# Output projection of a hybrid decoder layer: weight tiles loaded unsplit up to the fifth last, and split by ScalarE and GpSimd from the third quarter on

## The chip, the cores and the metric

The kernel runs on one core of one Trainium2 chip. The metric is the device time of one execution in microseconds; the time given for a kernel is the median of several executions. A second figure, the span, is the time from the first to the last instruction of the one execution that the hardware profiler recorded.

The engines are called TensorE (PE in the profile; PEld is its weight load), VectorE (DVE), ScalarE (ACT), GpSimd (POOL) and SyncE (SP, here the queue that issues the DMAs). In the code they are `PE`, `V`, `S`, `G` and `nc.sync`.

## The reference

One decoder layer over 2048 tokens of width 1024, in fp32. What matters here is its middle:

```python
mix = concatenate([o_a, o_b])                    # two token mixers, (2048, 1024)
mix_out = einsum('btc,cd->btd', mix, w_out)      # the output projection
h = h + rms_norm(mix_out, post_mix_norm)
u = einsum('btd,df->btf', rms_norm(h, pre_mlp_norm), w_mlp_up)
y = einsum('btf,fd->btd', square(relu(u)), w_mlp_down)
h = h + rms_norm(y, post_mlp_norm)
```

Ahead of it stand an input projection and the mixers (a gated DeltaNet and an HGRN2), behind it the MLP and a gated embedding of 256 inputs.

## The kernel before

Activations lie transposed, with 128 channels on the partitions. The 2048 tokens are cut into four quarters `q` of 512 (`QT`), the 1024 channels into eight blocks `d` of 128 (`KD = 8`).

**Precision by splitting.** A product in fp32 is made of three products of rounded halves. Each operand x is stored as a tile of two halves: half 0 is x rounded to the format fp32r, half 1 is x minus half 0, rounded too. `split` (L157 to L160) makes them: ScalarE copies (L159), then another engine subtracts (L160), which is VectorE in all the calls of the output projection. One output tile (q, d) is 8 blocks of channels times 3 terms, 24 matmuls of 128x128 by 128x512. The first two terms of a block use half 0 of the weights, the third uses half 1.

**Weights of the output projection.** `order` (L321) lists the 32 tiles (q, d), quarter by quarter; j counts them. Each tile needs the weights of its d, so each d's weights are used four times, once per quarter. They come in two ways. `stage_out(j)` (L324) loads the unsplit weights, 128x1024 fp32 or 512 KB, into a buffer tagged `raw`, of which there are two; `ready_out(j)` (L330) then splits them into a buffer tagged `whl`, of which there are three. Or, if nothing was staged for j, `ready_out(j)` calls `reload` (L178), a load of 1 MB of split weights from a copy in DRAM, which `keep` (L172) wrote in the first quarter. Before the change the first three quarters (`RAW = 3`, j = 0 to 23) take the first way and the last quarter (j = 24 to 31) the second; all eight d are kept in the first quarter.

**The loop.** At L1283 the kernel goes over `order`. At the head of pass j it calls

```python
ready_out(j + 2)
stage_out(j + 3)
```

so weights are loaded three tiles ahead and split two tiles ahead. In pass j = 27 (`len(order) - 5`) it allocates two more tiles tagged `raw`, called `u_raw`, and loads into them the first weights of the MLP; their splits (`w_u`) follow in the last passes. After the product of a tile ScalarE copies the accumulator out (`yo`, L1319) and squares it into a buffer `sq` that exists once (L222); VectorE adds the square up (`acc_o`, L223). Four accumulators (`pp`) take turns.

**Work between the tiles.** `mm` (L1085) counts matmuls, and every eighth calls `tick`, which runs what the agenda has for that moment. So the small steps are placed by TensorE's count, not by time. They are: the splits of the activations of the next quarters (`mixT`, L212 and L213); and, for each finished quarter, `normed` (L1169): the norm of the projected tile (`hl_o`, `nrm_o`, then Ln and Exp on ScalarE, `r_o`), then `residual` (L1148) with its eight steps on VectorE (`yo` L1159 and L1160, with `xo` loaded and `h1d` stored), the sum of squares of the result (`sq_h`, `acc_h`), and its norm (`hl_h`, `nrm_h` L1121 and L1122, `rn`). The offsets of these steps are

```python
OUT_STEPS = (1, 5) + tuple(range(7, 15)) + (15, 25)
```

so the last of them, with the matmul `nrm_h` of the second quarter, comes at the 25th tick after that quarter, 200 matmuls on. From the norm of the second quarter follow the operands of the MLP (`early_operands` L1211 with `be`, `up_operands` L1222 with `b` and `t`), which the first matmul `u` after the loop needs.

**Order on the engines.** TensorE's order is the program's (`manual_schedule`, L300). SP's order is the program's up to the first outs of this projection (L1002) and again in the MLP (L1335); within the loop, and on VectorE, ScalarE and GpSimd everywhere, the framework sorts the instructions at build time. Each engine then works through its own list in order.

Of the kernel before, what the change touches and what calls it, by code (L numbers as in the profile page):

```python
# [23 lines left out]
KD = D // P  # L24
# [59 lines left out]
def trunk(ctx, tc, x, xT, pT, vecs, w_in, w_ab, gdn_a_log, gdn_dt_bias, w_out, w_up, w_down,  # L84
          w_ple, w_gate, consts, out):
    nc = tc.nc
    V, S, G, PE = nc.vector, nc.scalar, nc.gpsimd, nc.tensor
# [69 lines left out]
    def split(t, eng, raw):  # L157

        S.activation(t[:, 0], raw, AF.Copy)  # L159
        eng.tensor_tensor(t[:, 1], raw, t[:, 0], ALU.subtract)  # L160
# [11 lines left out]
    def keep(key, w):  # L172

        c = dr.tile([P, 2 * KD * P], F32, name=f"cache_{key}")
        nc.sync.dma_start(c, w.bitcast(F32).rearrange("p h k n -> p (h k n)"))
        cached[key] = c

    def reload(key, name):  # L178
        w = wp.tile([P, 2, KD, P], F32R, tag="whl", name=f"w_{name}")
        nc.sync.dma_start(w.bitcast(F32).rearrange("p h k n -> p (h k n)"), cached[key])  # L180
        return w
# [137 lines left out]
            yield  # L319

    order = [(q, d) for q in range(NQ) for d in range(KD)]  # L321
    staged_out, ready, RAW = {}, {}, 3

    def stage_out(j):  # L324
        if j < len(order) and order[j][0] < RAW:
            raw = wp.tile([P, KD, P], F32, tag="raw", name=f"raw_out{j}", bufs=2)
            nc.sync.dma_start(raw, w_out[order[j][1]])
            staged_out[j] = raw

    def ready_out(j):  # L330
        if j >= len(order):
            return
        if j not in staged_out:
            ready[j] = reload(f"out{order[j][1]}", f"out{j}")
            return
        ready[j] = wp.tile([P, 2, KD, P], F32R, tag="whl", name=f"w_out{j}")
        split(ready[j], V, staged_out.pop(j))
        if order[j][0] == 0:
            keep(f"out{order[j][1]}", ready[j])

    clock, agenda = [0], {}
# [54 lines left out]
    with mixers as mctx:  # L396
# [605 lines left out]
        with tc.manual_schedule(engines={mybir.EngineType.SP}):  # L1002
# [29 lines left out]
            accs, store = {q: None for q in qs}, None  # L1032
            at(clock[0], mix_operands(0), (1, 2, 3, 4, 6, 7, 9, 11))
            call(clock[0] + 2, partial(stage_out, 0))
            call(clock[0] + 5, partial(ready_out, 0))
            call(clock[0] + 6, partial(stage_out, 1))
            call(clock[0] + 13, partial(ready_out, 1))
            call(clock[0] + 14, partial(stage_out, 2))
            held = {}

# [242 lines left out]
    for j, (q, d) in enumerate(order):  # L1283
        if d == 0:
# [3 lines left out]
            if q == 1:  # L1288
                later(mix_operands(3), range(17, 25))
        ready_out(j + 2)  # L1290
        stage_out(j + 3)
        if j == len(order) - 5:
# [441 lines left out]
```

## Time and profile before

| | |
|---|---|
| median of 3 runs | 2773.16 us (2772.43 to 2774.76) |
| the profiled execution | 2769.21 us, its span 2767.3 us |
| TensorE / VectorE / ScalarE / GpSimd busy | 97% / 74% / 53% / 4% of the span |
| mean granted TensorE clock | 0.993 of full speed |
| output projection: first to last matmul `mmo` | 1131.5 to 1327.1 us |
| `w_out` split by ScalarE / VectorE | 24 times, 1057 / 1224 ns median |

In the tables of stretches each engine's busy time stands with its count of instructions in this order: PE, PEld, DVE, ACT, POOL; then the granted clock of TensorE, the share of the DMA engines and GB/s. In a timeline a row has its start, its length, engine, line, operation, output and inputs, shape and count; in brackets the idle time of the engine before it and what ended that. Rows of consecutive like instructions are merged. A row of one tile's instructions gives the durations as minimum / median / maximum in ns. A row of waits gives the total in us, the times and the longest.

### The profile page before, as it was taken

The numbers are of one execution on the slowest core, as the hardware profiler recorded it, in microseconds if no ns is written. First come the engines' busy times: TensorE is split into PE (matmuls) and PEld (weight loads), VectorE is DVE, ScalarE is ACT, GpSimd is POOL, SyncE is SP. The second block draws the span as 40 slices with busy tenths as digits, with TensorE's granted clock in tenths as the row PEclk, the third lists the DMA queues.
The fourth block names the chain that finished last, engine by engine and source line by source line (L and its number), as shares of the span: only waits on it lengthen the run. The fifth ranks groups of instructions, "written<-read, shape, count | busy, mean of one in ns | idle before, by whom it ended". The sixth has DMA issues, their size and how long they took to land.

```text
span 2767.3 us, 38374 instructions
## 1 busy us (share of the span) xinstructions
PE 2680.7 (97%) x12721; PEld 2215.3 (80%) x12721; DVE 2044.9 (74%) x4242; ACT 1469.9 (53%) x2943; POOL 104.2 (4%) x104
## 2 busy tenths in 40 slices
PE   6999999999999999999999999999999999999999
PEld 4788788788888887777788888887888888887887
DVE  6788877787787677578889867857787765567775
ACT  6665555455546445575555646545454445465431
POOL 0000000000000000000000000001000000001000
PEclk9999999999999999999999999999999999999999
DMA  7776777667666665887466447667454356577663
GB/s 261 255 250 217 235 247 247 219 209 250 220 213 202 214 227 170 278 276 258 140 214 224 172 175 237 225 193 239 157 191 162 135 175 203 194 254 240 214 206 121
DMA packets 268598, 589.24 MB, mean 213 GB/s; under 512 B 55642, under 2 KB 59960, under 8 KB 249200
## 3 DMA queue, kind: packets, MB, share of 16 engines
q1 hardware_dynamic: 268400, 586.79, 63.6%
q8 instruction: 101, 1.65, 0.3%
q14 instruction: 97, 0.79, 0.1%
HBM read 419.75 MB, written 166.92 MB: 212 GB/s over the span
## 4 chain that ended last, share of the span: by engine, by line
PE 61%; DVE 15%; DMA 10%; issue 7%; ACT 4%; SPq 1%; POOL 1%; DVEq 0%; POOLq 0%; ACTq 0%
PE u L1090 22%; PE d L1090 20%; PE mm L1020 9%; PE mmg L1090 6%; DVE pr_g L658 2%; DMA ud_g<-u_g 2%; DMA sys_g<-ud_g 2%; DVE xs_g L661 1%; DVE xs_g L663 1%; PE mmo L1090 1%; DMA raw_out<-in_w_out_dram 1%; DVE xt L160 1%; DMA rd_g<-m_g 1%; DMA cache_in<-w 1%; DMA rsb_g<-rd_g 1%
## 5 line engine op out<-in xcount | busy, mean ns | idle before, releaser
L1020 PE MATMUL mm<-xt,w 128*128 128x512 f32 x3072 | 770.0, 399 | 3.3 <-ACT qk_h L758 1.6
L1020 PEld LDWEIGHTS mm<-xt,w 128*128 128x128 f32 x3072 | 559.5, 189 | 109.8 <-ACT qk_h L758 2.0
L1090 PE MATMUL d<-db,da 128*128 128x512 f32 x2688 | 615.3, 391 | 5.6 <-ACT db L212 3.7
L1090 PE MATMUL u<-t,wu 128*128 128x512 f32 x2604 | 603.7, 393 | 3.3 <-ACT wu L159 3.3
L1090 PEld LDWEIGHTS d<-db,da 128*128 128x128 f32 x2688 | 506.3, 189 | 113.9 <-ACT db L212 5.0
L1090 PEld LDWEIGHTS u<-t,wu 128*128 128x128 f32 x2604 | 488.7, 188 | 117.6 <-ACT wu L159 4.1
L213 DVE TENSOR_TENSOR db<-db 128x512 fp32r<-128x512 f32 x224 | 161.4, 720 | 75.2 <-ACT db L212 74.3
L1419 DVE TENSOR_TENSOR u<-u,u 128x512 f32<-128x512 f32 x224 | 150.3, 682 | 71.8 <-PE u L1090 70.6
L212 ACT ACTIVATE db<-db 128x512 fp32r<-128x512 f32 x224 | 140.8, 629 | 83.2 <-DMA db<-hid 77.8
L1090 PE MATMUL mmo<-mixT,w_out 128*128 128x512 f32 x720 | 171.7, 399 | 8.9 <-DVE w_out L160 6.4
L1090 PE MATMUL mmg<-h2T,wg 128*128 128x512 f32 x768 | 177.4, 393 | 0.0
L1460 ACT ACTIVATE u<-u 128x512 f32<-128x512 f32 x128 | 80.8, 632 | 176.4 <-DVE u L1419 176.1
L1090 PEld LDWEIGHTS mmo<-mixT,w_out 128*128 128x128 f32 x720 | 137.1, 191 | 42.5 <-DVE w_out L160 8.2
L1090 PEld LDWEIGHTS mmg<-h2T,wg 128*128 128x128 f32 x768 | 144.2, 188 | 32.9
L160 DVE TENSOR_TENSOR da<-da 128x512 fp32r<-128x512 f32 x128 | 93.0, 727 | 87.1 <-ACT da L159 86.9
L159 ACT ACTIVATE da<-da 128x512 fp32r<-128x512 f32 x128 | 80.4, 628 | 134.9 <-DMA da<-sumd 111.3
L159 ACT ACTIVATE wu<-a 128x512 fp32r<-128x512 f32 x124 | 73.9, 622 | 50.6 <-DMA a<-in_w_up_dram 49.2
L658 DVE TENSOR_TENSOR pr_g<-xs_g,sys_g 128x16 f32<-128x16 f32 (+14 forms) x240 | 93.8, 391 | 5.3
L223 POOL TENSOR_TENSOR acc_y<-acc_y,sq_y 128x512 f32<-128x512 f32 x28 | 38.5, 1374 | 1392.8 <-ACT sq_y L222 1392.0
L160 DVE TENSOR_TENSOR wu<-a,wu 128x512 fp32r<-128x512 f32 x124 | 84.7, 686 | 3.6 <-ACT wu L159 3.5
L1461 ACT ACTIVATE u<-u 128x512 f32<-128x512 f32 x128 | 80.8, 631 | 3.7
L160 DVE TENSOR_TENSOR da<-dr,da 128x512 fp32r<-128x512 f32 x96 | 66.2, 690 | 18.5 <-ACT da L159 16.8
(374 smaller groups left out, 3800.9 us busy)
## 6 DMA issues: line engine op xcount, KB each, us to landing
w<-cache_in SPq DMA_DIRECT2D x96, 1024.0 KB
db<-hid SPq DMA_DIRECT2D x224, 256.0 KB
cache_in<-w SPq DMA_DIRECT2D x32, 1024.0 KB
hid<-u SPq DMA_DIRECT2D x128, 256.0 KB
da<-sumd SPq DMA_DIRECT2D x128, 256.0 KB
a<-in_w_up_dram SPq DMA_DIRECT2D x124, 256.0 KB
hid<-ht SPq DMA_DIRECT2D x96, 256.0 KB
dr<-in_w_down_dram SPq DMA_DIRECT2D x96, 256.0 KB
```

Source lines behind the costliest of these rows:

```text
L159: S.activation(t[:, 0], raw, AF.Copy)
L160: eng.tensor_tensor(t[:, 1], raw, t[:, 0], ALU.subtract)
L212: S.activation(t[:, 0], plain(t), AF.Copy)
L213: V.tensor_tensor(t[:, 1], plain(t), t[:, 0], ALU.subtract)
L223: eng.tensor_tensor(acc, acc, sq, ALU.add)
L658: V.tensor_tensor(pr[:, :, :, 0:i], xs[:, None, :, 0:i].broadcast_to([P, 2, GC, i]), sys[:, 0:i, i : i + 2].rearrange("p j two -> p two j" ...
L661: V.tensor_reduce(xs[:, :, i : i + 2].rearrange("p g two -> p two g"), pr[:, :, :, 0 : i + 1], AX.X, ALU.add)
L1020: PE.matmul(ps, *terms[i], start=i == 0, stop=i == nt - 1)
L1090: PE.matmul(ps, a, b, start=start, stop=stop)
L1419: V.tensor_tensor(c[new], c[old], ps, ALU.add)
L1460: S.activation(c[k], c[k], AF.Relu)
L1461: S.activation(c[k], c[k], AF.Square)
```

## The change

The unsplit way now serves j = 0 to 26, all but the last five tiles; `RAW` counts tiles instead of quarters. In the first quarter only the weights that are reloaded later are kept, d = 3 to 7. The subtraction of the split stays on VectorE in the first two quarters and is done by GpSimd from j = 16 on, eleven times.

```diff
-    staged_out, ready, RAW = {}, {}, 3
+    staged_out, ready, RAW = {}, {}, len(order) - 5
 
     def stage_out(j):
-        if j < len(order) and order[j][0] < RAW:
+        if j < RAW:
             raw = wp.tile([P, KD, P], F32, tag="raw", name=f"raw_out{j}", bufs=2)
             nc.sync.dma_start(raw, w_out[order[j][1]])
             staged_out[j] = raw
...
         ready[j] = wp.tile([P, 2, KD, P], F32R, tag="whl", name=f"w_out{j}")
-        split(ready[j], V, staged_out.pop(j))
-        if order[j][0] == 0:
+        split(ready[j], V if order[j][0] < 2 else G, staged_out.pop(j))
+        if order[j][0] == 0 and order[j][1] >= RAW % KD:
             keep(f"out{order[j][1]}", ready[j])
```

## The prediction

> **What bounds the kernel now.** I read the page's head first, then the waits of TensorE in the stretch of the output projection, then TensorE's own timeline there.
>
> ```profile
> span 2767.3 us, 38374 instructions
> PE 2680.7 (97%) x12721; PEld 2215.3 (80%) x12721; DVE 2044.9 (74%) x4242; ACT 1469.9 (53%) x2943; POOL 104.2 (4%) x104
> ```
>
> TensorE is busy for 97% of the span, so a change beside it can only win back its pauses. GpSimd (POOL) is almost unused, and that is where the change puts work.
>
> ```profile
> PE mmo L1090 <- DVE w_out L160: 5.9, 3, 3.1
> PE u L1090 <- ACT w_u L159: 3.5, 1, 3.5
> PE mmo L1090 <- ACT sq_o L222: 1.9, 1, 1.9
> ```
>
> These are TensorE's waits from 1224 to 1345 us (total, times, longest). Three pauses, 5.9 us together, end with VectorE's half of a weight split (DVE w_out L160), the instruction that the change moves. The timeline (start, length, count, idle before) places them:
>
> ```profile
> 1226.73 2.13 PE L1090 MATMUL mmo<-mixT,w_out 128*128 128x512 f32 x8 [1.86 <-ACT sq_o L222]
> 1251.33 5.85 PE L1090 MATMUL mmo<-mixT,w_out 128*128 128x512 f32 x24 [0.59 <-DVE w_out L160]
> 1259.39 7.38 PE L1090 MATMUL mmo<-mixT,w_out 128*128 128x512 f32 x24 [2.21 <-DVE w_out L160]
> 1269.86 14.37 PE L1090 MATMUL mmo<-mixT,w_out 128*128 128x512 f32 x54 [3.09 <-DVE w_out L160]
> 1284.07 0.39 PE L1121 MATMUL nrm_h<-hl_h,ones 128*128 128x512 f32 x1
> 1336.50 6.60 PE L1090 MATMUL u<-t,w_u 128*128 128x512 f32 x16 [3.50 <-ACT w_u L159]
> ```
>
> A tile is 24 matmuls. Counting them from the third quarter's first at 1226.73, the pauses lie two matmuls into j = 20, 21 and 22: those two use ScalarE's half of the weights, the third needs the other half. The pauses also cost something after they end: the tile begun at 1259.39 takes 7.38 us for the same 24 matmuls that took 5.85 us before it. The stretches say why (PEclk stands third from the end):
>
> ```profile
> 1259.30:1261.00 1.70, 1.61 (x5) 1.33 (x6) 1.70 (x4) 1.03 (x2) 0.00 (x0) 0.70 0.96 280
> 1261.00:1263.00 2.00, 2.00 (x6) 1.51 (x6) 2.00 (x5) 0.56 (x2) 0.00 (x0) 0.50 0.84 258
> 1263.00:1265.00 2.00, 2.00 (x10) 1.60 (x9) 2.00 (x5) 0.74 (x2) 0.00 (x0) 0.90 0.95 363
> 1269.80:1272.00 2.20, 2.14 (x6) 1.72 (x7) 2.20 (x5) 0.60 (x1) 0.00 (x0) 0.60 0.94 383
> 1272.00:1274.00 2.00, 2.00 (x7) 1.58 (x6) 2.00 (x4) 0.63 (x1) 0.00 (x0) 0.59 1.05 403
> ```
>
> After the pauses of 2.21 and 3.09 us the granted clock is near half. Length times (1 - PEclk) gives 0.5 + 1.0 + 0.2 = 1.7 us after the first and 0.9 + 0.8 = 1.7 us after the second. So late weights cost 5.9 + 3.4 = 9.3 us, which is the most that the moved splits can win directly.
>
> The Trainium skill, "TensorE: Matmul & The Clock Gate", Part 1, puts the return to half clock after an idle window of about 3.4 us. By that figure neither pause would have lost clock, and the prize would be 5.9 us; the rows show the loss after 2.21 us, so I keep 9.3.
>
> Why the splits are late: VectorE has no room. In these stretches the third busy column is DVE's.
>
> ```profile
> 1237.00:1250.00 13.00, 13.00 (x58) 10.54 (x57) 7.97 (x13) 12.70 (x17) 0.00 (x0) 1.00 0.42 150
> 1250.00:1265.00 15.00, 12.20 (x46) 9.13 (x45) 15.00 (x24) 7.29 (x12) 0.00 (x0) 0.89 0.69 220
> 1265.00:1280.00 15.00, 11.91 (x45) 9.29 (x44) 12.24 (x18) 6.20 (x10) 0.00 (x0) 0.89 0.80 263
> 1245.27 1.05 ACT L159 ACTIVATE w_out<-raw_out 128x1024 fp32r<-128x1024 f32 x1
> 1250.06 1.22 DVE L160 TENSOR_TENSOR w_out<-raw_out,w_out 128x1024 fp32r<-128x1024 f32 x1
> ```
>
> From 1250 to 1265 VectorE is busy throughout. ScalarE finished its half of j = 20 at 1246.32, and VectorE took up the other half 3.7 us later.
>
> **The change, part by part.**
>
> ```profile
> L159 ACT ACTIVATE w_out<-raw_out x24: 1042/1057/1065, 1101.2 to 1265.0; 128x1024 fp32r<-128x1024 f32 x24
> L160 DVE TENSOR_TENSOR w_out<-raw_out,w_out x24: 1215/1224/1227, 1102.3 to 1273.5; 128x1024 fp32r<-128x1024 f32 x24
> L175 SPq DMA_DIRECT2D cache_out<-w_out x8: 319/320/402, 1103.8 to 1169.7; - x8
> L180 SPq DMA_DIRECT2D w_out<-cache_out x8: 319/327/403, 1266.5 to 1311.0; - x8
> ```
>
> *Three stores to the cache fewer* (d = 0, 1, 2 of the first quarter): three issues of 0.32 us on the SP queue and 3 MB written. TensorE's waits in the output projection name no store and no load of these tiles; I cost this at nothing. *Three reloads become unsplit loads* (j = 24 to 26): 512 KB instead of 1 MB, plus three ScalarE copies of 1.06 us. ScalarE is busy 6.20 of 15 us from 1265 to 1280, which hides 3.2 us; and no pause of TensorE before was put down to a reload. Nothing again, or 3.2 us if that cover were gone. The unsplit loads keep both raw buffers occupied until the split of j = 26, so the two `u_raw` tiles start later; the split of j = 26 comes about when the matmul of 1284.07 does, which leaves some 50 us of cover before the u matmul of 1336.50.
>
> *Eight splits leave VectorE and eleven go to GpSimd.* VectorE loses 8 instructions of 1.22 us. GpSimd's price is not in the trace at this size. The nearest row is its sum of 128x512:
>
> ```profile
> L223 POOL TENSOR_TENSOR acc_y<-acc_y,sq_y x28: 1285/1298/1688, 1740.6 to 2590.1; 128x512 f32<-128x512 f32 x28
> ```
>
> Twice the size cannot take less than this row's 1.3 us; twice the median is 2.6 and twice the longest 3.4. I take 2.45, a little under the doubled median, since some of each instruction is paid once whatever its size.
>
> The Trainium skill, "GPSIMD Engine Reference", 3.1, has 4497 ns for a two-input fp32 operation on 2048 elements, against VectorE's 2293; half of it, 2.25 us, is an estimate from that page, and the sum below would be 1.2 us smaller by it.
>
> What matters is what VectorE does meanwhile:
>
> ```profile
> 1870.32 1.30 POOL L223 TENSOR_TENSOR acc_y<-acc_y,sq_y 128x512 f32<-128x512 f32 x1 [123.69 <-ACT sq_y L222]
> 1870.04 1.88 DVE L1523 TENSOR_TENSOR y<-y,d 128x512 f32<-128x512 f32 x3
> 1872.37 1.30 POOL L223 TENSOR_TENSOR acc_y<-acc_y,sq_y 128x512 f32<-128x512 f32 x1 [0.74 <-ACT sq_y L222]
> 1871.83 0.69 DVE L160 TENSOR_TENSOR da<-da 128x512 fp32r<-128x512 f32 x1
> 1872.85 1.37 DVE L213 TENSOR_TENSOR db<-db 128x512 fp32r<-128x512 f32 x1 [0.33 <-ACT db L212]
> ```
>
> The DVE operation of 1871.83, with both inputs in SBUF, takes 0.69 us; its like at 1872.85, begun inside a GpSimd operation, takes 1.37, that is, it finishes 0.69 us after 1873.53, close to GpSimd's end at 1873.67. At 1870.04 three operations with one input in PSUM run through at full speed beside GpSimd. (Operations in a queue overlap a little: the one of 1871.83 starts 0.09 us before the group of 1870.04 ends, so a split removed frees 1.22 - 0.09 = 1.13 us of VectorE.) So a GpSimd operation holds VectorE's two-SBUF-input work until about 0.14 us before its own end. The Trainium skill, "SBUF — State Buffer", "Who interferes with whom", states this as a rule, a shared port held for the whole instruction, and it speaks against the change: nearly all of VectorE's work in this stage (residual sums, squares, splits) has two SBUF inputs.
>
> By the rows, then, each split holds VectorE for 2.45 - 0.14 = 2.3 us where it has work, instead of 1.13: the busy engine is not relieved but loaded by 1.2 us more. What is won is that weights no longer stand in VectorE's queue: GpSimd can begin as soon as ScalarE's half is done, at most one DVE operation later, and the pauses at j = 20 to 22 go.
>
> What is late next is the norm of the second quarter. Its matmul has a fixed place in TensorE's order, 8 matmuls into j = 24, and needs `hl_h`, the last link of a chain of residual sums on VectorE:
>
> ```profile
> 1277.98 0.69 DVE L223 TENSOR_TENSOR acc_h<-acc_h,sq_h 128x512 f32<-128x512 f32 x1 [2.04 <-ACT sq_h L222]
> 1280.03 0.69 DVE L223 TENSOR_TENSOR acc_h<-acc_h,sq_h 128x512 f32<-128x512 f32 x1 [0.76 <-ACT sq_h L222]
> 1281.39 0.69 DVE L223 TENSOR_TENSOR acc_o<-acc_o,sq_o 128x512 f32<-128x512 f32 x1 [0.67 <-ACT sq_o L222]
> 1282.00 0.68 DVE L160 TENSOR_TENSOR hl_h<-acc_h,hl_h 128x512 fp32r<-128x512 f32 x1
> ```
>
> It is done at 1282.7 and TensorE comes at 1284.07: 1.4 us of slack. Without late weights TensorE would come at 1284.07 - 9.3 = 1274.8. VectorE, without its pauses of 2.04 + 0.76 + 0.67 = 3.5 us and four splits of 1.13 = 4.5 us, would have `hl_h` at 1274.7, about the same. But five GpSimd splits (j = 20 to 24) fall into that stretch. With four of them meeting a busy VectorE, 4 x 2.3 = 9.2 us come on top: 1283.9 us, that is -0.2 against 1284.07. TensorE gives back at the norm what it won at the weights.
>
> Earlier, at the border of the second and third quarter, VectorE is just as full:
>
> ```profile
> 1215.42 1.05 ACT L159 ACTIVATE w_out<-raw_out 128x1024 fp32r<-128x1024 f32 x1
> 1223.48 1.22 DVE L160 TENSOR_TENSOR w_out<-raw_out,w_out 128x1024 fp32r<-128x1024 f32 x1
> 1226.08 0.60 ACT L222 ACTIVATE sq_o<-mmo 128x512 f32<-128x512 f32 x1 [0.76 <-DVE acc_h L223]
> ```
>
> TensorE's 1.86 us pause before 1226.73 ends with this square, which frees an accumulator and itself waits for VectorE. The splits of j = 16 (from 1216.5) and j = 17 come ahead of it: 2 x (2.3 - 1.13) = 2.3 us more, 0 if they fall in pauses. The splits of j = 25 and 26 come after the norm, where VectorE waits for ScalarE's root; 0 to 1 us at the 3.50 us wait of u, and I take 0.5.
>
> The sum is -0.2 + 2.3 + 0.5 = +2.6 us. The profiled execution took 2769.21 us (span 2767.3 and 1.9 around it), 3.95 us (0.14%) under the median 2773.16; carried onto the median, that is 2775.8, say 2776. Bounds of this case: with two of five splits costing and none at the border, about -5; with all five and 1 us at u, 2.1 + 2.3 + 1 = +5.4.
>
> **The rivals.** *The splits fall into VectorE's pauses, or its order is re-sorted around them* (the DVE, ACT and SP orders here are the compiler's). For it: 5.0 us of idle in the 13 us from 1237. Against: 15.00 busy of 15 from 1250. Then the whole 9.3 us is won: 2764.
>
> *GpSimd's hold is longer than the row suggests, and VectorE's chain decides outright.* The split writes another type (fp32r) than `acc_y` does, and that row goes up to 1.69 us. At 3.4 us a split holds VectorE 3.3; five put `hl_h` at 1291.2 (+7.1), two at the border add 4.3, u 1: +12, or 2785. With all splits counted the change goes from gain to loss at a hold of about 1.7 us (1274.7 + 5h - 1284.07 + 2(h - 1.13) = 0) and past 0.2% at about 2.5.
>
> *The change does not do what it says*: the weights are late all the same, because GpSimd's longer split frees the raw buffers no earlier and the loads follow late. Then pauses of about the old size remain, about 2773. Against it: the 3.7 us that j = 20 queued for VectorE exceed GpSimd's extra 1.2.
>
> **How the numbers follow.** A measurement of this kernel can tell about 0.2%, 5.5 us, from no change. Forecast (+2.6, -5 to +5.4, and a little beyond for a re-sorted order): 0.50, split into 0.33 within, 0.14 slower, 0.03 faster. All won: 0.22, of it 0.20 faster. Long hold: 0.23, slower. Nothing changed: 0.05, within. Together faster 0.23, within 0.40, slower 0.37. The range takes in most of both rivals: 2765 to 2785.
>
> **What would show it.** Right: `w_out` on POOL eleven times at 2.3 to 2.6 us; no TensorE wait on it; DVE operations of two SBUF inputs stretched by 1 to 2 us beside them; a new TensorE wait at nrm_h (L1121) of several us for `hl_h`; the sq_o wait at the border grown. Wrong: DVE operations unstretched (then the first rival), POOL splits over 3 us (the second), or TensorE still waiting for `w_out` (the third).

## The result, and the profile after

| | before | after | ratio after / before, 95% |
|---|---|---|---|
| median of the runs beside each other (14 each) | 2774.01 us (2771.34 to 2780.02) | 2779.95 us (2773.11 to 2786.96) | 1.0020 [1.0010, 1.0029] |
| the same kernel run again later (12 runs, before 35) | 2773.09 us | 2777.18 us (2770.91 to 2781.57) | 1.0015 [1.0006, 1.0025] |

The change costs 4 to 5.5 us: a little slower, at the edge of the 0.2% that can be told from no change. The forecast was 2776.0 us, 2.8 us over the median of 2773.16 that it started from, in a range of 2765 to 2785.

The profiled execution of the changed kernel was the longest of its fourteen (2786.96 us, span 2785.2), so mechanisms are read from it, and times from the profile of the second set, whose execution of 2776.69 us (span 2774.9) is near its median.

The head of the page, changed kernel:

```profile
span 2785.2 us, 38386 instructions
PE 2690.3 (97%) x12721; PEld 2218.5 (80%) x12721; DVE 2059.3 (74%) x4234; ACT 1472.8 (53%) x2946; POOL 138.5 (5%) x115
```

VectorE has eight instructions fewer (4242 to 4234) and yet is busy longer (2044.9 to 2059.3 us). TensorE has the same 12721 matmuls and 9.6 us more busy time: it ran some of them at a lower clock, as the stretches below show. The instructions on tile `w_out` (ns minimum / median / maximum):

```profile
L160 DVE TENSOR_TENSOR w_out<-raw_out,w_out x16: 1215/1225/1226, 1109.4 to 1221.4; 128x1024 fp32r<-128x1024 f32 x16
L160 POOL TENSOR_TENSOR w_out<-raw_out,w_out x11: 2392/2547/6704, 1223.6 to 1298.7; 128x1024 fp32r<-128x1024 f32 x11
L175 SPq DMA_DIRECT2D cache_out<-w_out x5: 319/320/833, 1147.2 to 1172.6; - x5
L180 SPq DMA_DIRECT2D w_out<-cache_out x5: 336/424/675, 1302.0 to 1324.4; - x5
```

GpSimd does ten of its eleven splits in 2.39 to 3.32 us each; one took 6.70. The first store to the cache comes 43 us later than before (1103.8) and the first reload 35 us (1266.5), of which 7 us are only a later start of this whole part in this execution. TensorE's waits from 1090 to 1380 us, those of the tile loop and of u:

```profile
PE mmo L1090 <- ACT sq_o L222: 11.2, 4, 5.3
PE mmo L1090 <- DMA w_out<-cache_out: 4.4, 2, 4.2
PE u L1090 <- ACT w_u L159: 3.3, 1, 3.3
...
PE mmo L1090 <- POOL w_out L160: 0.7, 1, 0.7
```

The 5.9 us of waits for VectorE's half are gone; 0.7 us are left for GpSimd's. In their place the wait for the square `sq_o`, which frees an accumulator, grew from 1.9 to 11.2 us, and a wait for reloads has come. The timeline round the longest new pause, on GpSimd, VectorE, ScalarE and TensorE:

```profile
1277.66 3.03 POOL L160 TENSOR_TENSOR w_out<-raw_out,w_out 128x1024 fp32r<-128x1024 f32 x1 [5.26 <-ACT w_out L159]
1277.82 0.68 DVE L1160 TENSOR_TENSOR yo<-yo,xo 128x512 f32<-128x512 f32 x1
1278.42 2.82 DVE L1159 SCALAR_TENSOR_TENSOR yo<-yo,cols,r_o 128x512 f32<-128x512 f32 x1
1281.17 0.68 DVE L1160 TENSOR_TENSOR yo<-yo,xo 128x512 f32<-128x512 f32 x1
1281.77 0.68 DVE L223 TENSOR_TENSOR acc_h<-acc_h,sq_h 128x512 f32<-128x512 f32 x1
1282.48 0.60 ACT L222 ACTIVATE sq_o<-mmo 128x512 f32<-128x512 f32 x1 [3.26 <-DVE acc_h L223]
1283.13 10.27 PE L1090 MATMUL mmo<-mixT,w_out 128*128 128x512 f32 x32 [5.29 <-ACT sq_o L222]
```

Read it downwards. A GpSimd split runs from 1277.66 to 1280.69. VectorE's first `yo` operation in it still runs at full speed; the second takes 2.82 us where its like takes 0.74. Two operations later comes `acc_h`, which empties the one buffer `sq`; only then can ScalarE square the accumulator (it waited 3.26 us), and only then has TensorE an accumulator to write. After the pause 32 matmuls take 10.27 us; at the rate of 24 in 5.85 they would take 7.8. The stretches say it is the clock (third from the end):

```profile
1233.90:1237.30 3.40, 3.38 (x9) 2.71 (x10) 3.34 (x4) 2.52 (x4) 3.40 (x1) 0.55 0.03 12
1283.10:1285.00 1.90, 1.87 (x4) 1.49 (x5) 1.19 (x2) 1.63 (x3) 0.00 (x0) 0.50 0.84 289
1285.00:1287.00 2.00, 2.00 (x6) 1.61 (x5) 2.00 (x3) 1.05 (x2) 1.51 (x1) 0.50 0.82 257
```

The first of them follows the pause at the border of the second and third quarter. TensorE, GpSimd and VectorE there:

```profile
1223.13 3.48 DVE L1160 TENSOR_TENSOR yo<-yo,xo 128x512 f32<-128x512 f32 x2
1223.64 2.42 POOL L160 TENSOR_TENSOR w_out<-raw_out,w_out 128x1024 fp32r<-128x1024 f32 x1 [60.23 <-ACT w_out L159]
1231.19 9.52 POOL L160 TENSOR_TENSOR w_out<-raw_out,w_out 128x1024 fp32r<-128x1024 f32 x2 [5.13 <-ACT w_out L159]
1233.92 3.49 PE L1090 MATMUL mmo<-mixT,w_out 128*128 128x512 f32 x8 [3.96 <-ACT sq_o L222]
1234.36 0.68 DVE L223 TENSOR_TENSOR acc_o<-acc_o,sq_o 128x512 f32<-128x512 f32 x1
1234.96 0.68 DVE L160 TENSOR_TENSOR hl_h<-acc_h,hl_h 128x512 fp32r<-128x512 f32 x1
1235.70 2.74 DVE L223 TENSOR_TENSOR acc_o<-acc_o,sq_o 128x512 f32<-128x512 f32 x1
```

The same tile began after a pause of 1.86 us before, now after 3.96, and its 8 matmuls take 3.49 us instead of 2.13.

To place the time, I cut the part round the projection at marks on TensorE: the first matmul `mme` of the stage ahead, the first `mmo`, the first `nrm_h` (8 matmuls into the third quarter), the second `nrm_h` (8 into j = 24), the first `u`, the first `u` of the next weights `wu`. The marks before that were not shown yet:

```profile
1083.82 1.61 PE L186 MATMUL mme<-pT,w_pleb 128*128 128x512 f32 x6
1131.76 1.99 PE L1048 MATMUL mmo<-mixT,w_out 128*128 128x512 f32 x8
1228.70 0.40 PE L1121 MATMUL nrm_h<-hl_h,ones 128*128 128x512 f32 x1
1327.34 5.66 PE L1090 MATMUL u<-t,w_u 128*128 128x512 f32 x24
1354.58 6.14 PE L1090 MATMUL u<-t,wu 128*128 128x512 f32 x24 [0.77 <-ACT wu L159]
```

and those of the second profile of the changed kernel, with its pauses:

```profile
1088.64 1.61 PE L186 MATMUL mme<-pT,w_pleb 128*128 128x512 f32 x6
1135.14 1.99 PE L1048 MATMUL mmo<-mixT,w_out 128*128 128x512 f32 x8
1230.74 3.62 PE L1090 MATMUL mmo<-mixT,w_out 128*128 128x512 f32 x8 [3.99 <-ACT sq_o L222]
1234.16 0.50 PE L1121 MATMUL nrm_h<-hl_h,ones 128*128 128x512 f32 x1
1280.06 10.25 PE L1090 MATMUL mmo<-mixT,w_out 128*128 128x512 f32 x32 [5.32 <-ACT sq_o L222]
1290.14 0.50 PE L1121 MATMUL nrm_h<-hl_h,ones 128*128 128x512 f32 x1
1318.99 16.83 PE L1090 MATMUL mmo<-mixT,w_out 128*128 128x512 f32 x72 [0.64 <-DMA w_out<-cache_out]
1335.66 5.66 PE L1090 MATMUL u<-t,w_u 128*128 128x512 f32 x24
1363.97 6.15 PE L1090 MATMUL u<-t,wu 128*128 128x512 f32 x24 [0.77 <-ACT wu L159]
```

Differences of these starts, and of the same marks in the other kernels' profiles (one profiled execution each, us):

| kernel | ahead | to border | third quarter | tail | u | sum |
|---|---|---|---|---|---|---|
| before | 47.9 | 96.9 | 55.4 | 43.3 | 27.2 | 270.8 |
| after | 45.4 | 100.6 | 56.0 | 50.3 | 26.4 | 278.7 |
| after, second profile | 46.5 | 99.0 | 56.0 | 45.5 | 28.3 | 275.3 |
| e1 loads only | 45.8 | 98.2 | 54.3 | 44.1 | 29.8 | 272.1 |
| e2 GpSimd only | 47.2 | 98.6 | 55.7 | 43.3 | 28.4 | 273.1 |
| e3 two halves | 45.8 | 99.9 | 54.9 | 45.5 | 29.1 | 275.2 |
| e4 twice | 46.5 | 102.2 | 74.4 | 44.3 | 28.5 | 295.9 |
| e5 idle reads | 47.8 | 96.2 | 63.8 | 43.3 | 26.9 | 278.0 |
| e6 idle writes | 48.6 | 95.9 | 56.5 | 43.3 | 27.7 | 271.9 |
| e7 reload from 20 | 48.0 | 95.8 | 52.4 | 43.3 | 29.3 | 268.7 |
| e8 reload from 16 | 48.1 | 96.7 | 55.5 | 43.3 | 27.2 | 270.9 |
| e10 GpSimd from 20 | 46.2 | 96.9 | 60.1 | 44.0 | 28.3 | 275.5 |
| e11 GpSimd to 19 | 45.7 | 99.7 | 53.6 | 43.3 | 28.7 | 271.0 |
| e12 four parts | 45.9 | 100.5 | 53.1 | 45.2 | 30.1 | 274.8 |

From before to the second profile of after: -1.4, +2.1, +0.6, +2.2, +1.1, together +4.6 us, which is what the ratio 1.0015 makes of 2773.09 us (+4.2). The spans differ by 7.6; the rest lies in stages that the change doesn't touch. The two profiles of after differ by up to 1.9 us in four of the columns and by 4.8 in the tail, so a single line says little; the groups of lines say more.

### The profile page after: what moved, and what is told of

It reads as the page before. It is cut to its first block, busy times and chain, and to the rows that moved or that the text cites. A ratio compares the mean times of both kernels' runs of the same rounds, so it can differ in the third digit from the quotient of the medians.

```text
span 2785.2 us, 38386 instructions
## 1 busy us (share of the span) xinstructions
PE 2690.3 (97%) x12721; PEld 2218.5 (80%) x12721; DVE 2059.3 (74%) x4234; ACT 1472.8 (53%) x2946; POOL 138.5 (5%) x115
## 4 chain that ended last, share of the span: by engine, by line
PE 54%; DVE 10%; DMA 7%; issue 5%; ACT 2%; SPq 1%; POOL 1%; DVEq 0%; POOLq 0%; ACTq 0%
PE u L1090 21%; PE d L1090 19%; PE mmg L1090 6%; PE mm L1020 5%; DMA sys_g<-ud_g 1%; DMA ud_g<-u_g 1%; DVE pr_g L658 1%; DVE xs_g L661 1%; DMA rsb_g<-rd_g 1%; DVE xs_g L663 1%; DMA rd_g<-m_g 1%; DMA da<-sumd 1%; DVE acc_o L223 0%; DVE yo L1160 0%; PE mmo L1090 0%
## 5 line engine op out<-in xcount | busy, mean ns | idle before, releaser
L1090 PE MATMUL mmo<-mixT,w_out 128*128 128x512 f32 x720 | 174.4, 402 | 16.3 <-ACT sq_o L222 11.2
L159 ACT ACTIVATE wu<-a 128x512 fp32r<-128x512 f32 x124 | 73.9, 622 | 50.5 <-DMA a<-in_w_up_dram 47.8
L663 DVE SCALAR_TENSOR_TENSOR xs_g<-xs_g,sys_g 128x4 f32<-128x4 f32 x256 | 57.9, 226 | 29.6 <-DMA sys_g<-ud_g 24.5
```

Source lines behind the costliest of these rows:

```text
L663: V.scalar_tensor_tensor(xs[:, :, i + 1], xs[:, :, i], sys[:, i, i + 1 : i + 2], xs[:, :, i + 1], ALU.mult, ALU.add)
L1090: PE.matmul(ps, a, b, start=start, stop=stop)
```

## The experiments

The theory: a GpSimd operation that reads SBUF holds back VectorE's operations with two inputs in SBUF, so the splits load VectorE's chain more than they relieve it, and the accumulators come free late. Rivals: the loads are to blame (three more unsplit ones, and the reloads behind them); GpSimd's own slowness is (weights late because a split takes 2.5 us instead of 1.2); or writing to SBUF, not reading, is what disturbs. Ratios are to the kernel before in runs beside it on the same chip, with 95% intervals; times are medians.

### e1: the loads without GpSimd

```diff
-        split(ready[j], V if order[j][0] < 2 else G, staged_out.pop(j))
+        split(ready[j], V, staged_out.pop(j))
```

> The new loads (27 unsplit tiles, five kept) with every split on VectorE. Theory H (GpSimd's split holds VectorE): without GpSimd the cost of the change is gone; three more VectorE splits of 1.13 us fall into a full stretch, so 0 to +4 us against the kernel before, VectorE's operations keep their 0.69 us, TensorE waits for w_out as before. Theory L (the cost is in the loads: the last raw buffers delay the two u_raw loads, and the reloads stand behind those in SP's order, 4 us of TensorE wait in the changed kernel): the reload wait of about 4 us is seen here too, +4 to +9 us.

Measured: 2770.28 us, 0.9995 [0.9985, 1.0004]. TensorE's waits in the loop:

```profile
PE mmo L1090 <- DVE w_out L160: 5.9, 2, 4.6
...
PE mmo L1090 <- ACT sq_o L222: 3.0, 2, 2.4
```

The loads and stores alone cost nothing that can be measured. The late weights are there, as long as before.

### e2: GpSimd without the loads

The kernel before, `RAW = 3` quarters, with GpSimd's subtraction for j = 16 to 23.

```diff
-        split(ready[j], V, staged_out.pop(j))
+        split(ready[j], V if order[j][0] < 2 else G, staged_out.pop(j))
```

> The loads of the kernel before (24 unsplit tiles, all kept, eight reloads), with the eight splits of the third quarter on GpSimd. H: nearly the whole cost of the change, +2 to +8 us against before; VectorE's two-input operations beside a split take 2 to 3 us; TensorE's waits move from w_out to the squares that free accumulators. L: the moved splits by themselves only win, -5 to -9 us.

Measured: 2775.35 us, 1.0008 [0.9998, 1.0019]. The waits changed as in the full change:

```profile
PE mmo L1090 <- ACT sq_o L222: 9.2, 2, 5.3
...
PE mmo L1090 <- POOL w_out L160: 0.8, 1, 0.8
```

So the exchange of one wait for the other comes from GpSimd alone; its net price, about 2 us, is within the noise of this measurement.

### e3: each GpSimd split in two halves

```diff
-        split(ready[j], V if order[j][0] < 2 else G, staged_out.pop(j))
+        raw = staged_out.pop(j)
+        if order[j][0] < 2:
+            split(ready[j], V, raw)
+        else:
+            S.activation(ready[j][:, 0], raw, AF.Copy)
+            for i in range(2):
+                sl = slice(i * KD // 2, (i + 1) * KD // 2)
+                G.tensor_tensor(ready[j][:, 1, sl], raw[:, sl], ready[j][:, 0, sl], ALU.subtract)
```

> The changed kernel with each GpSimd subtraction cut into two of 128x512 each. The total held is about the same (2 x 1.3 us), but VectorE can get in between. H, if only the total counts: as the changed kernel within 3 us. H, if the length of a single hold counts: 2 to 6 us faster than it. L: no difference.

Measured: 2773.84 us, 1.0003 [0.9995, 1.0012]. The longest `yo` operation on VectorE falls from 2.89 to 1.78 us, so the hold goes with the length of the GpSimd instruction. In time it is 6.1 us less than the whole change by the medians, but the two were measured beside different runs and their intervals overlap; TensorE still waits 11.9 us for `sq_o`.

### e4: each GpSimd split done twice

The second subtraction repeats the first, with the same result.

```diff
+        raw = staged_out.pop(j)
-        split(ready[j], V if order[j][0] < 2 else G, staged_out.pop(j))
+        split(ready[j], V if order[j][0] < 2 else G, raw)
+        if order[j][0] >= 2:
+            G.tensor_tensor(ready[j][:, 1], raw, ready[j][:, 0], ALU.subtract)
```

> The changed kernel with each GpSimd subtraction done twice, the second over the same data. Weights are 2.4 us later, which the lead of two tiles covers. H: another 2.3 us of hold for each of six to eleven splits, +10 to +22 us against the changed kernel. L: within 3 us of the changed kernel.

Measured: 2797.49 us, 1.0094 [1.0081, 1.0107], some 20 us over the changed kernel. TensorE's waits:

```profile
PE mmo L1093 <- ACT sq_o L222: 18.4, 6, 6.2
PE mmo L1093 <- POOL w_out L340: 7.0, 2, 3.5
```

Beyond the change the price rises steeply, mostly through VectorE's chain (18.4 us), but GpSimd's own lateness shows too (7.0). Since both act here, this run alone doesn't say which of the two mattered at the single dose.

### e5: idle reads on GpSimd, the kernel before otherwise

VectorE splits as before; GpSimd then adds the raw tile to itself, for no use.

```diff
-        split(ready[j], V, staged_out.pop(j))
+        raw = staged_out.pop(j)
+        split(ready[j], V, raw)
+        if order[j][0] == 2:
+            G.tensor_tensor(raw, raw, raw, ALU.add)
```

> The kernel before, its splits on VectorE, and behind each split of the third quarter an idle GpSimd sum of the raw tile with itself (128x1024, reads and writes SBUF, used by nobody). It moves no work and delays no weights; it only keeps GpSimd reading eight times, and each raw buffer some 2.5 us longer. H (GpSimd's reads hold VectorE): VectorE's two-input operations beside it take 2 to 3 us, +6 to +16 us against before (the second subtraction of the last set cost 18 us for eleven). If the cost was in when weights come, not in the hold: 0 to +3.

Measured: 2777.84 us, 1.0016 [1.0005, 1.0028]. The tile `yo` on VectorE:

```profile
L1162 DVE SCALAR_TENSOR_TENSOR yo<-yo,cols,r_o x16: 740/743/2382, 1200.8 to 1283.4; 128x512 f32<-128x512 f32 x16
```

### e6: idle writes in their place

```diff
+        raw = staged_out.pop(j)
-        split(ready[j], V, staged_out.pop(j))
+        split(ready[j], V, raw)
+        if order[j][0] == 2:
+            for _ in range(2):
+                G.memset(raw, 0.0)
```

> The same with two GpSimd memsets of the raw tile in place of the sum: GpSimd is about as busy and holds the raw buffer about as long, but reads nothing. H: VectorE's operations keep 0.69 us, 0 to +3 us against before. If any GpSimd work, or the later raw buffer, is what costs: as with the idle sums.

Measured: 2771.61 us, 0.9993 [0.9983, 1.0002]. The same tile, and GpSimd's instructions on the raw tile:

```profile
L1163 DVE SCALAR_TENSOR_TENSOR yo<-yo,cols,r_o x16: 743/748/753, 1200.7 to 1274.7; 128x512 f32<-128x512 f32 x16
...
L341 POOL MEMSET raw_out<- x16: 952/954/962, 1225.3 to 1277.7; 128x1024 f32 x16
```

The pair shows what stretches VectorE: beside the sums, which read, its `yo` operation takes up to 2.38 us, beside the memsets, which only write, it stays at 0.75. The first kernel costs 4.4 us, the second nothing. The Trainium skill, "SBUF — State Buffer", "Who interferes with whom", says that a VectorE instruction with two inputs in SBUF contends with a GpSimd instruction that reads SBUF, and not with one that only writes; these two runs agree.

The pair doesn't isolate the cost as well as the stretch. From e5:

```profile
1230.74 9.27 POOL L340 TENSOR_TENSOR raw_out<-raw_out 128x1024 f32<-128x1024 f32 x2 [4.23 <-DVE w_out L160]
...
PE mmo L1093 <- DVE w_out L160: 12.5, 4, 6.3
```

Two of the sums took 9.27 us together, where a pair of memsets takes 1.96 to 1.98, so some raw buffers were held longer too. And TensorE's added wait stands at VectorE's splits (12.5 us, 7.5 in e6), not at `sq_o` (1.6 us) as in the change. The 4.4 us lie between the two ranges that were expected.

### e7 and e8: no late splits on any engine

The kernel before with fewer unsplit tiles: the tiles from j = 20 (e7) or j = 16 (e8) on are reloaded from the cache, so that neither VectorE nor GpSimd splits them.

```diff
-    staged_out, ready, RAW = {}, {}, 3
+    staged_out, ready, RAW = {}, {}, 20
...
-        if j < len(order) and order[j][0] < RAW:
+        if j < RAW:
```

> The kernel before with the four tiles that were late (j = 20 to 23) reloaded as split weights instead of split again: 2 MB more to load, four splits of 1.13 us fewer on VectorE and four of 1.06 us fewer on ScalarE, and no GpSimd. If VectorE's room is the limit, the pauses at w_out go and nothing holds VectorE: -4 to -9 us against before. If the loads are the limit: the pauses come back as waits for the reload, -1 to +5.

> As the last, with all eight tiles of the third quarter reloaded (j = 16 to 31): eight splits fewer on VectorE, 4 MB more to load. If VectorE's room is the limit: -5 to -12 us against before, the wait for the squares at j = 16 shorter too. If the loads are: 0 to +8.

Measured: e7 2770.63 us, 0.9990 [0.9978, 1.0001]; e8 2768.82 us, 0.9991 [0.9982, 1.0000]. By the ratios that is -2.8 and -2.5 us, less than was expected of either if VectorE's room were the limit (-4 to -9 and -5 to -12). TensorE in e7:

```profile
1276.70 10.03 PE L1090 MATMUL mmo<-mixT,w_out 128*128 128x512 f32 x32 [3.68 <-ACT yo L1319]
```

and in e8:

```profile
1274.39 15.24 PE L1090 MATMUL mmo<-mixT,w_out 128*128 128x512 f32 x56 [7.76 <-DMA w_out<-cache_out]
```

This sizes the prize. Without any late split the third quarter of e7 is 3.0 us shorter than before, not 9.3: TensorE runs into the accumulators instead and waits for ScalarE to copy one out (the square just ahead of that copy had waited 1.27 us for VectorE's `acc_o`). In e8 the reload itself comes late.

### e9: the change again

The changed kernel, unaltered, beside the next three on one chip; its result is in the first table.

> The changed kernel, unaltered, beside the next three on the same chip, and a second profile of it. Expected: +4 to +8 us against before, as measured. H: the waits for the squares at the border and at the end of the residual sums are there again, about 4 and 5 us; the 4 us wait for a reload, if it hangs on the run, may be gone.

Its queue of DMAs and GpSimd explain the tail:

```profile
1295.65 2.41 POOL L160 TENSOR_TENSOR w_out<-raw_out,w_out 128x1024 fp32r<-128x1024 f32 x1 [3.57 <-ACT w_out L159]
1298.09 0.80 SPq L1297 DMA_DIRECT2D u_raw<-in_w_up_dram  x2
1298.94 0.42 SPq L180 DMA_DIRECT2D w_out<-cache_out  x1
```

The last split ends at 1298.06; only then is its raw buffer free for the two loads into the second `u_raw` tile, issued from 1298.09 on; and the first reload of the projection stands behind them in SP's queue. TensorE then waits for reloads twice, 1.1 us in all.

### e10: GpSimd from j = 20 on

```diff
-        split(ready[j], V if order[j][0] < 2 else G, staged_out.pop(j))
+        split(ready[j], V if j < 20 else G, staged_out.pop(j))
```

> The changed kernel with j = 16 to 19 split by VectorE; GpSimd takes only j = 20 to 26. My sum had 2.3 us for the border (j = 16 and 17) and -0.2 for the rest of the stretch. By it: 2 to 4 us faster than the changed kernel, the wait for the squares at the border back to about 2 us; the wait later in the third quarter unchanged.

Measured: 2774.18 us, 1.0009 [0.9998, 1.0020]. That is 3.0 us under the change beside it, as the sum had it, but the intervals overlap. The pause at the border is back to 2.06 us.

### e11: GpSimd for j = 16 to 19 only

```diff
-        split(ready[j], V if order[j][0] < 2 else G, staged_out.pop(j))
+        split(ready[j], G if 16 <= j < 20 else V, staged_out.pop(j))
```

> The complement: GpSimd takes only j = 16 to 19, VectorE j = 20 to 26. By my sum the border costs +2.3 us and the late weights stay, so +2 to +5 us against before; by H the waits of 4 us at the border and for w_out at j = 20 to 22 stand side by side.

Measured: 2770.01 us, 0.9990 [0.9981, 1.0000], against +2 to +5 us expected. The waits:

```profile
PE mmo L1090 <- ACT sq_o L222: 4.6, 2, 4.0
PE mmo L1090 <- DVE w_out L160: 4.3, 1, 4.3
```

The intervals of e9 and e11 do not touch: the splits from j = 20 on cost 7 us between these two kernels. Those at the border cost a longer pause (3.95 us instead of e1's 2.42), but not the whole time: the weights of j = 20 to 22 are then late by 4.3 us instead of 5.9, since TensorE comes later to them. e10 shows the same from the other side: without the longer pause at the border its third quarter takes 60.1 us, four more than the full change's. TensorE pays for VectorE's backlog once, at the one place or the other, so the terms don't add up one by one.

### e12: each GpSimd split in four parts

As e3, with `range(4)` and quarters of the tile.

> The changed kernel with each GpSimd subtraction cut into four of 128x256. In two halves it was 6 us faster than the changed kernel's own measurement, on another chip. If the length of a single hold counts: as the halves or up to 3 us better, that is 4 to 9 us faster than the changed kernel beside it. If the halves' gain was scatter, or GpSimd's fixed part per instruction eats it: within 3 us of the changed kernel or slower.

Measured: 2775.28 us, 1.0011 [1.0001, 1.0021]. The longest `yo` operation is down to 1.23 us, but the four instructions (1182 ns median instead of about 640 for a quarter of 2547) keep GpSimd longer, and TensorE still waits 10.8 us for `sq_o`. In quarters the time doesn't come back: 1.9 us less than the change beside it, within the noise, and not the 4 to 9 expected if the single hold counted. Whether the halves' 1.0003 was scatter stays open. In the traces a whole split stretches one VectorE operation by some 2.1 us, a half by some 1.0 and a quarter by some 0.5, so the total per split is about the same; that this is why nothing is won is a likely reading, not a shown one.

## Why the prediction was right

**The late weights go: right.** 5.9 us of waits for VectorE's half became 0.7 for GpSimd's.

**GpSimd's price, 2.45 us: right.** 2392 minimum, 2547 median. **The hold, 2.3 us against 1.13 freed: right, a little large.** A split that met a busy VectorE stretched one operation, most by 2.0 to 2.2 us: from 0.68 or 0.74 us to as much as 2.9. e5 and e6 show that it is the reading.

**"At most one DVE operation later": wrong for one of the eleven.** At the border GpSimd was given two splits from 1231.19 on, and the first of them took 6.70 us. VectorE ran its own two-input operations back to back until `hl_h` ended at 1235.64, and the next one, at 1235.70, was the first to be stretched. So a waiting GpSimd instruction can be passed over by several of VectorE's operations; in the second profile the same pair took 9.50 us. What decides is not shown: the split of 1277.66 was let in after one operation, though VectorE's followed without a gap there too. The late weights themselves brought TensorE no wait at the border.

**"A new TensorE wait at nrm_h for hl_h": right chain, wrong place.** TensorE stops one step earlier, at the accumulator: with one `sq` buffer ScalarE's squares wait for VectorE's sums, and the square of the projected tile stands behind that of the residual. `nrm_h` itself waits for nothing any more, because TensorE has already lost the time. A second `sq` buffer would test this link directly; that was not tried, and so it rests on the rows shown.

**Third quarter, -0.2: the size right, in part by luck.** It is +0.6 us. `hl_h` ends 55.3 us behind the first `nrm_h` in both profiles of after, where the sum gives 1283.9 - 1228.7 = 55.2. But the sum took four holds of 2.3 us, 9.2 together. In the trace the seven splits of j = 18 to 24 each stretch an operation ahead of `hl_h`, by 14.3 us together (14.0 in the second profile). Without any split in that quarter (e8) `hl_h` ends 47.9 us behind the mark, so by an estimate from these figures some 7 of the 14 us fell where VectorE would have paused.

**The clock behind the new pauses: left out.** The sum charged 3.4 us of clock to the pauses that go and none to those that come. In the second profile the 8 matmuls behind the pause at the border take 3.62 us instead of 2.13, and the 32 behind that of 1280.06 take 10.25 instead of 7.8. That is 3.9 us, nearly as much as the whole change costs.

**The border, +2.3: the size right, the working only in part.** The pause grew by 2.1 us, and the matmuls behind it took 1.4 to 1.5 more; up to the mark the two profiles of after are 3.6 and 2.1 us longer than before's. In the table six profiles with the splits of j = 16 and 17 on GpSimd once (after twice, e2, e3, e11, e12) have a mean of 99.7 us up to the border, the seven others (without e4) 96.7; the groups do not overlap. But the sum put two holds ahead of the pause, and the rows show one. The split of j = 16 stretches the second `yo` of the pair at 1223.13; that of j = 17 first holds the operation of 1235.70, when the pause had ended at 1233.92. One hold of 2.1 us less two freed splits of 1.13 comes to about nothing. VectorE's order changed as well: from the first matmul of j = 10 to the square that ends the pause it makes 12 `mixT` splits in both profiles of after and in e11, but 8 in before and 9 in e1 and e10. No run separates that order from the hold.

**"9.3 us, the most that the moved splits can win": a bound, but no prize.** e7 took the same pauses away without GpSimd, and got 3.0 us in that quarter. The 9.3 left out that the accumulators are late by themselves a little later. So the first rival's 2764 was out of reach even without a hold.

**"Three reloads become unsplit loads … Nothing again": the term that was mis-sized.** The tail grew by 2.2 us in the second profile and by 7.0 in the first, where one wait for a reload took 4.17 us. The prediction saw that `u_raw` would start later, and asked only who waits for `u_raw`; it didn't ask what stands behind those loads on SP's queue. e1 (the same loads, VectorE's shorter splits: 44.1), e2 (GpSimd, no such loads: 43.3) and e11 (the late splits on VectorE: 43.3) have a shorter tail than after's 45.5, e3's 45.5 and e12's 45.2; e10 (44.0) and e4 (44.3), which ought to have the long one too, do not. So it varies with the execution, and the rows of e9 are its mechanism.

**"Three stores … at nothing": wrong, to the good side.** In the eight profiles with three stores fewer the stage ahead takes 45.4 to 46.5 us, in the six with all eight 47.2 to 48.6. The mean differs by 2.0 us. By the rows, the first stores fell into that stage before (1103.8 us) and come after it now (1147.2). No run changed the stores alone, so their part is inferred.

**u, +0.5:** its wait was 3.5 us before and is 3.3 or 5.4 now; not settled.

Together: forecast +2.6; by the second profile +4.6, that is, the two terms with a mechanism (+2.1) came out at +2.7, and the tail, the stage ahead and u, costed at +0.5, at +1.9. That the number is so near is luck as well: the stage ahead (-1.4) and the tail (+2.2), both costed at nothing, offset each other in part. The rival of a long hold fails on GpSimd's 2.5 us, the one of weights late all the same on the 0.7 us. No kernel tried here beats the kernel before by more than 0.1%.

## What to carry to other kernels

When an operation is moved from a full VectorE to an idle GpSimd, compare what it frees with how long it holds VectorE's two-input work: here 1.13 against some 2.1 us, and an idle engine's help was a loss. Before a pause is counted as a prize, ask which resource the engine would reach next if it were gone; a kernel that removes the work altogether (e7) shows how much of it is really there. And of a load that moves later, follow the queue behind it, not its own user alone.

## What the runs showed of the hardware

- GpSimd's 128x1024 subtraction waited through some 4 us of VectorE's back-to-back operations and was counted as one instruction of 6.70 us (6.69 in the second profile, 6.70 in e11). Others were let in after one operation or at once; no run shows what decides.
- A whole split mostly stretched one VectorE operation, by 2.0 to 2.2 us; a half by some 1.0, a quarter by some 0.5. It need not have two inputs in SBUF: in e4 the one-input TENSOR_SCALAR `rr_h` took 2.61 us beside a split, and 0.42 elsewhere.
- How long a pause of TensorE must be to cost clock is not fixed. At the border a pause of 2.06 us (e10) was followed by 8 matmuls in 3.59 us, one of 2.42 (e1) by 3.68, but one of 2.46 (e8) by the undisturbed 2.13. The Trainium skill, "TensorE: Matmul & The Clock Gate", Part 1, has a free-running window of about 3.4 us, which would make it a matter of phase; the spread agrees with that, while pauses well under 3.4 us did cost clock.
- The price of cutting a GpSimd operation: 2547 ns whole, 2 x 1740 in halves, 4 x 1182 in quarters (medians beside a busy VectorE; minima 2392, 1292 and 732).
